# First block's modulation sums on TensorE, small vectors on the weights' queue, and w_in chunks issued a chunk ahead

## The chip, the cores and the metric

The kernel runs on one core of a Trainium2 chip. The metric is device time in microseconds. TensorE is called PE, VectorE DVE, ScalarE ACT, GpSimdE POOL, and SyncE, which issues most DMAs, SP.

## What is computed

One layer of a streaming encoder for 256 tokens of width 2048, in float32. Cut to what matters here:

```python
mod = silu(c) @ ada_w + ada_b                    # 2048 -> 6 x 2048
shift1, scale1, gate1, shift2, scale2, gate2 = split(mod)
h = rmsnorm(x, norm1_g) * (1 + scale1) + shift1
proj = h @ w_in                                  # 2048 -> 9216
u, v, q, k, v_b, gates = split(proj)
y_a = spatial_gating(gelu(u), gelu(v), gmlp_w_s, gmlp_b_s, ...) @ w_branch_a
y_b = band_attention(q, k, v_b, rel_bias) @ w_branch_b
x = x + gate1 * ((sigmoid(gates_a) * y_a + sigmoid(gates_b) * y_b) @ w_out)
h = rmsnorm(x, norm2_g) * (1 + scale2) + shift2
x = x + gate2 * moe(h)                           # 32 SwiGLU experts, two for each token
out = rmsnorm(x, final_g)
```

## The kernel before

The stages come in this order: a start (small vectors, x, its norm and transposes), the first part of the projection (five targets q, k, v_b, v, u of 1024 columns), the gates of the projection, the two branches, the output projection, the router, and the experts, whose weights (12.6 MB each) stream in one after the other.

The first part goes in four blocks (`BLOCKS = (4, 4, 4, 4)`). A block is four groups of 128 rows of w_in, because `h` can only be made for the columns whose shift and scale are known. In a block, `run_steps` is called for each of the five targets: it loads one chunk of w_in (128 x 4 x 1024, 2 MB, L111) and makes four steps. A step splits 128 x 1024 weights into a high part (ACT, L318) and a low part (DVE, L319), each in one of two buffers, and makes 12 products of 512 columns (L292 high x high, L293 low x high, L294 high x low). A block has 20 steps, 240 products. The partial results are copied (first block, ACT, L351) or added (DVE, L353).

While the products of one block run, the modulations of the next block are made by the generator `ada_block`, of which `run_steps` takes one step at each chunk and at each split (25 calls a block, 23 steps of the generator). It loads 2048 rows of ada_w, the shift and scale columns of the block, in four pieces of 2 MB (two DMAs each, L195), multiplies them with silu(c) and accumulates on DVE (L205 once, L207 15 times), sums over the partitions by transposes on PE and a reduce on DVE (L217, L220), adds the biases (L223 to L225), and makes `hx`, its high part `hh` and its low part `hl` (L230, L233 on ACT, L234 on DVE). The modulations of the first block are made by the same code ahead of the first chunk.

All these loads take the buffers r0 to r3 in turn (`raws`), and SP issues them one after the other; a load waits until the work on the load four before it is done. In the program a block's order is chunk, piece, chunk, piece, chunk, piece, chunk, piece, chunk. The order of instructions on an engine is set by a scheduler that goes by a model of when each is ready; it need not be the program's order, except where `issue_after` or `keep_in_program_order` says so.

In the last block the modulations of the rest (`ada_units`, L435) run in the place of `ada_block`. The router's stage holds a sum over one half of the last gate that is made by PE alone (`gate_steps`, L990): float32 matmuls with 64 equal columns of silu(c) as stationary operand and 512 columns of ada_w as moving one, two of them for two halves of the partitions of one bank. The experts' products are L1279, L1361 and L1393.

At the start c, norm1_g, two rows of ada_b and gmlp_b_s go by ACT's queue into one tile `rows` that PE turns (L169, L171), x goes by the same queue in two halves (L164), gmlp_w_s by POOL's (L167) and is turned ahead of the first block (L269, L270). ACT squares x (L251), scales it (L254) and copies the transposes of x (L259) to `hx` (L264).

Of the kernel before, what the change touches and what calls it, by code (L numbers as in the profile page):

```python
# [17 lines left out]
P = 128  # L18
S = 256
# [27 lines left out]
def hybrid_block(  # L47
# [69 lines left out]
    pending = []  # L117

# [22 lines left out]

    ident = T([P, P], "ident")
# [8 lines left out]
    rows = T([P, P], "a2")  # L151
    nc.vector.memset(rows, 0.0)
    r0 = 0
# [12 lines left out]
    for i in range(2):  # L166
        nc.gpsimd.dma_start(out=ws[i], in_=gmlp_w_s[0, 4 * i : 4 * i + 4].rearrange("g t s -> t g s"))  # L167
# [5 lines left out]
    nc.scalar.activation(sc, cols[:, 0:ND], AF.Silu)  # L173
# [13 lines left out]
    def ada_block(k0, n):  # L187

        w = n * P
        acc = accs.sb([P, 2, w])  # L190
        nj = 16 // n
        for j0 in range(0, ND, nj):
            rw = raws.sb([P, nj, 2, w])
            for m in range(2):
                nc.sync.dma_start(  # L195
                    out=rw[:, :, m, :],
                    in_=ada_w[
                        0, j0 * P : (j0 + nj) * P, m * D + k0 * P : m * D + k0 * P + w
                    ].rearrange("(j p) n -> p j n", p=P),
                )  # L200
            yield
# [12 lines left out]
        for m in range(2):  # L214
# [8 lines left out]
        nc.vector.tensor_add(sh1[:, ks], sums[:, 0, :], b_shift[:, ks])  # L223
        nc.vector.tensor_add(sg1[:, ks], sums[:, 1, :], b_scale[:, ks])
        nc.vector.scalar_tensor_tensor(  # L225
            out=sg1[:, ks], in0=sg1[:, ks], scalar=1.0, in1=g1c[:, ks], op0=ALU.add, op1=ALU.mult
        )
        yield
        for j in range(k0, k0 + n):
# [5 lines left out]
            if j % 2 == 1:  # L235
                yield

# [9 lines left out]
    first = ada_block(0, BLOCKS[0])  # L247
    ss1 = T([P, NT], "ss1")
    scr = T([P, D], "e2")
    for t in range(NT):  # L250
        nc.scalar.activation(scr, xt[t], AF.Square, accum_out=ss1[:, t : t + 1])  # L251
    rs1 = inv_rms(ss1, "n1")
    for t in range(NT):
        nc.scalar.activation(xt[t], xt[t], AF.Copy, scale=rs1[:, t : t + 1])  # L254
    for j in range(0, ND, 2):
        tp = bk.ps()
# [7 lines left out]
        nc.scalar.copy(hx[:, j : j + 2, :], tp.rearrange("p (a b) -> p a b", a=2))  # L264
    wsT = T([P, 8, P], "f3")
    for i in range(2):
        tp = bk.ps()
        for g in range(4):
            nc.tensor.transpose(tp[:, g * P : (g + 1) * P], ws[i][:, g, :], ident)  # L269
        nc.scalar.copy(wsT[:, 4 * i : 4 * i + 4, :], tp.rearrange("p (a b) -> p a b", a=4))  # L270
    nc.gpsimd.memset(wsT[CH:P, :, 0:CH], 0.0)
    for _ in first:
        pass


    def run_steps(lh, ll, w, k0, n, c0, evac, with_ada=None, cw=CW, after=None):

        nhf = cw // 512
        npc = 4096 // cw
        pt = []  # L280
# [24 lines left out]
        for q in range(k0, k0 + n, npc):  # L305
            m = min(npc, k0 + n - q)
            rw = load([P, m, cw], w[q * P : (q + m) * P, c0 : c0 + cw].rearrange("(j p) n -> p j n", p=P))
            if with_ada is not None:
                next(with_ada, None)
            for jj in range(m):  # L310
# [6 lines left out]
                def prepare(wh=wh, wl=wl, src=rw[:, jj, :]):  # L317
                    nc.scalar.copy(wh, src)  # L318
# [175 lines left out]
    for b, n in enumerate(BLOCKS):  # L494
        lastb = b == len(BLOCKS) - 1
        nxt = ada if lastb else ada_block(k0 + n, BLOCKS[b + 1])
# [7 lines left out]
        for c0, dst, func in homes:  # L504
            done = lastb and c0 == homes[-1][0]
            run_steps(
                lh_h, ll_h, win, k0, n, c0, home_evac(dst, func, b == 0, lastb), with_ada=nxt,
                after=(lambda: sides.append(both())) if done else None,
            )
        if not lastb:  # L510
            for _ in nxt:
                pass
        k0 += n
# [1091 lines left out]
```

## Time and profile before

| | us |
|---|---|
| median of 3 runs (1688.21 to 1690.66) | 1690.38 |
| the profiled execution's own time | 1689.86 |
| its span | 1688.1 |
| PE busy, share of the span | 1538.8, 91% |
| DVE busy | 942.5, 56% |
| ACT busy | 483.5, 29% |
| first product of the first block (L292) | 44.92 |

The span goes from the first to the last instruction of the profiled execution; its own time has 1.8 us around it. A busy share is an average over stages that have different limits.

### The profile page before, as it was taken

How to read it: one execution, taken by the hardware profiler on the slowest of the kernel's cores; microseconds unless marked ns; L12 is line 12 of the kernel's file. 1: busy time of each engine (PE TensorE's matmuls, PEld its weight loads, DVE VectorE, ACT ScalarE, POOL GpSimd, SP SyncE). 2: the span in 40 equal slices, each digit the busy share in tenths (PEclk: the TensorE clock that was granted, in tenths of full speed). 3: DMA queues.
4: the chain of work that ended last, by engine and by line, in shares of the span. 5: the costliest groups of instructions: out<-in, count | busy, mean ns of one | idle time of the engine just before them, and what ended most of it. 6: DMA issues, size and time to landing. Idle time of an engine off the chain costs nothing.

```text
span 1688.1 us, 18245 instructions
## 1 busy us (share of the span) xinstructions
PE 1538.8 (91%) x6725; PEld 856.1 (51%) x6725; DVE 942.5 (56%) x1313; ACT 483.5 (29%) x785; POOL 126.3 (7%) x377
## 2 busy tenths in 40 slices
PE   2999999999999999999998989989899898898996
PEld 1777778777887776643333323334233333332432
DVE  5789999998778888734332333323333233332334
ACT  4554345675444345341110111101111011110112
POOL 1000000000000000011100101001011010100101
PEclk8999999999999999999999999999999999999998
DMA  9989897797988786899999999999999999999996
GB/s 359 343 315 341 336 341 299 296 343 273 351 313 315 305 312 244 343 384 418 416 418 417 416 418 416 417 418 416 418 416 418 418 416 418 416 417 417 416 419 245
DMA packets 135358, 625.25 MB, mean 370 GB/s; under 512 B 5720, under 2 KB 5840, under 8 KB 101856
## 3 DMA queue, kind: packets, MB, share of 16 engines
q1 hardware_dynamic: 132832, 614.49, 91.5%
q10 hardware_dynamic: 992, 5.28, 0.8%
q0 software_dynamic: 1440, 4.27, 0.8%
q8 instruction: 55, 0.90, 0.2%
q14 instruction: 39, 0.32, 0.0%
HBM read 621.91 MB, written 2.10 MB: 370 GB/s over the span
## 4 chain that ended last, share of the span: by engine, by line
PE 51%; DMA 42%; DVE 4%; issue 2%; ACT 1%; SPq 0%; POOL 0%; POOLq 0%; DVEq 0%; ACTq 0%
DMA r<-in_w_dram 22%; PE b L1279 12%; PE b L294 11%; PE b L292 11%; PE b L293 10%; DMA dC<-in_w_dram 9%; DMA E<-in_w_dram 8%; PE b L1361 3%; DMA r<-in_ada_w_dram 2%; DVE W L319 1%; DVE f L435 1%; PE b L1393 1%; DVE f L207 0%; PE b L1183 0%; PE b L593 0%
## 5 line engine op out<-in xcount | busy, mean ns | idle before, releaser
L1279 PE MATMUL b<-r,e 128*64 128x512 f32 x1024 | 376.3, 626 | 44.2 <-DMA r<-in_w_dram 43.6
L1395 DVE TENSOR_TENSOR dB<-dB,b 128x512 f32<-128x512 f32 x248 | 153.6, 681 | 317.4 <-PE b L1393 317.4
L318 ACT CAST W<-r 128x1024 fp32r<-128x1024 f32 (+1 forms) x224 | 220.8, 987 | 328.6 <-PE b L293 294.0
L319 DVE TENSOR_TENSOR W<-r,W 128x1024 fp32r<-128x1024 f32 (+1 forms) x224 | 255.8, 1147 | 64.5 <-ACT W L318 63.2
L292 PE MATMUL b<-W,dC 128*128 128x512 f32 x704 | 284.9, 405 | 5.3 <-ACT dC L233 3.7
L293 PE MATMUL b<-W,dD 128*128 128x512 f32 x704 | 280.0, 398 | 0.0
L294 PE MATMUL b<-W,dC 128*128 128x512 f32 x704 | 267.1, 398 | 2.3 <-DVE W L319 2.1
L1385 ACT CAST f<-f 64x512 fp32r<-64x512 f32 x124 | 76.4, 616 | 576.2 <-DVE dB L1395 414.2
L1279 PEld LDWEIGHTS b<-r,e 128*64 128x64 f32 x1024 | 116.7, 144 | 215.9 <-issue 144.1
L292 PEld LDWEIGHTS b<-W,dC 128*128 128x128 f32 x704 | 132.9, 189 | 40.8 <-ACT dC L233 4.1
L294 PEld LDWEIGHTS b<-W,dC 128*128 128x128 f32 x704 | 131.5, 188 | 38.9 <-DVE W L319 8.0
L435 DVE SCALAR_TENSOR_TENSOR f<-r,sc,f 128x1024 f32<-128x1024 f32 x115 | 147.2, 1281 | 4.5 <-DMA r<-in_ada_w_dram 3.7
L293 PEld LDWEIGHTS b<-W,dD 128*128 128x128 f32 x704 | 132.7, 189 | 30.4 <-issue 0.5
L1279 PE MATMUL b<-dC,e 128*64 128x512 f32 x256 | 120.0, 624 | 19.6 <-DMA dC<-in_w_dram 19.6
L1279 PE MATMUL b<-E,e 128*64 128x512 f32 x256 | 118.2, 616 | 19.4 <-DMA E<-in_w_dram 19.4
L1279 PE MATMUL b<-dD,e 128*64 128x512 f32 x256 | 127.2, 648 | 0.0
L1352 DVE TENSOR_TENSOR f2y<-f2y,b 128x256 f32<-128x256 f32 x31 | 13.1, 421 | 198.6 <-ACT f2y L1351 198.6
L1279 PE MATMUL b<-W,e 128*64 128x512 f32 x256 | 121.8, 625 | 0.0
L1361 PE MATMUL b<-r,f2y 128*64 128x512 f32 x496 | 111.3, 595 | 0.0
L1386 DVE TENSOR_TENSOR f<-f,f 64x512 fp32r<-64x512 f32 x124 | 85.1, 686 | 26.4 <-ACT f L1385 23.5
L1294 POOL COPY e<-a 128x64 f32 x256 | 68.7, 271 | 205.0 <-PE b L1279 191.1
L207 DVE SCALAR_TENSOR_TENSOR f<-r,sc,f 128x1024 f32<-128x1024 f32 x60 | 77.0, 1283 | 1.6 <-DMA r<-in_ada_w_dram 1.0
(321 smaller groups left out, 1475.5 us busy)
## 6 DMA issues: line engine op xcount, KB each, us to landing
r<-in_w_dram SPq DMA_DIRECT2D x93, 2048.0 KB, 28.2
r<-in_w_in_dram SPq DMA_DIRECT2D x36, 2048.0 KB, 8.4
r<-in_ada_w_dram SPq DMA_DIRECT2D x32, 2048.0 KB, 8.6
W<-in_w_dram SPq DMA_DIRECT2D x23, 2048.0 KB, 28.5
dC<-in_w_dram SPq DMA_DIRECT2D x23, 2048.0 KB
dD<-in_w_dram SPq DMA_DIRECT2D x23, 2048.0 KB, 28.2
E<-in_w_dram SPq DMA_DIRECT2D x23, 2048.0 KB, 28.1
r<-in_ada_w_dram SPq DMA_DIRECT2D x32, 1024.0 KB, 10.1
```

Source lines behind the costliest of these rows:

```text
L207: nc.vector.scalar_tensor_tensor(out=acc, in0=rw[:, jj], scalar=sc[:, j : j + 1], in1=acc, op0=ALU.mult, op1=ALU.add,)
L292: nc.tensor.matmul(o, a, wh[:, cs], start=(k == k0), stop=False)
L293: nc.tensor.matmul(o, b, wh[:, cs], start=False, stop=False)
L294: closed[0] = nc.tensor.matmul(o, a, wl[:, cs], start=False, stop=close)
L318: nc.scalar.copy(wh, src)
L319: nc.vector.tensor_sub(wl, src, wh.bitcast(F32))
L435: nc.vector.scalar_tensor_tensor(out=acc, in0=rw[:, jj, :], scalar=sc[:, j : j + 1], in1=acc, op0=ALU.mult, op1=ALU.add,)
L1279: nc.tensor.matmul(pab[a * CH : (a + 1) * CH, :], xe[:, 8 * half + j, :], w[:, j // JQ, j % JQ, :], start=(half == 0 and j == 0), stop=(ha ...
L1361: nc.tensor.matmul(po[a * CH : (a + 1) * CH, :], act[:, j, :], w[:, j, a * 512 : (a + 1) * 512], start=(j == 0), stop=(j == 3),)
L1385: pin(nc.scalar.copy(oh[r, a, :], og[r, b, :]))
L1386: pin(nc.vector.tensor_sub(oh[o, a, :], og[r, b, :], oh[r, a, :].bitcast(F32)))
L1395: pin(nc.vector.tensor_add(xa[:, t, d0 : d0 + 512], xa[:, t, d0 : d0 + 512], pr))
```

## The change

The first block's sums are made by PE alone, in the manner of L990 (`ada_first`): silu(c), repeated in 64 columns, is the stationary operand, a piece of ada_w the moving one, and shift and scale land in two halves of one bank. The sums are then equal on 64 partitions; a matmul with a two-column `pick` turns them into columns. `hh` is made from `hx` directly by one ACT pass, `hl` by two DVE passes, the first group of 128 rows ahead of the other three.

c, norm1_g and ada_b (in one DMA) go first on SP's queue, gmlp_b_s on POOL's, x first on ACT's. x is scaled by DVE, the copies of its transposes alternate between ACT and DVE and use six banks. A Silu of two elements stands ahead of the real one.

The first quarter of the first w_in chunk is loaded ahead of the first block's last piece, the rest behind it. In the first part each chunk is issued one chunk earlier in the program, ahead of the piece of modulations beside it (`follow`, `fetched`). gmlp_w_s is loaded (by ACT's queue) and turned after the first block, beside the products of the second (`turn_ws`, one step at each step of products).

```diff
@@ start
+    casts = []
+    fetched = []
...
-    for src in (
-        c[0].rearrange("(j p) -> j p", p=P),
-        norm1_g[0].rearrange("(j p) -> j p", p=P),
-        ada_b[0, 0:D].rearrange("(j p) -> j p", p=P),
-        ada_b[0, D : 2 * D].rearrange("(j p) -> j p", p=P),
-        gmlp_b_s[0],
-    ):
-        nc.scalar.dma_start(out=rows[r0 : r0 + src.shape[0], :], in_=src)
-        r0 += src.shape[0]
     for t in range(NT):
         nc.scalar.dma_start(out=xt[t], in_=x[0, t * P : (t + 1) * P, :])
-    ws = [T([P, 4, P], "a0"), T([P, 4, P], "a1")]
-    for i in range(2):
-        nc.gpsimd.dma_start(out=ws[i], in_=gmlp_w_s[0, 4 * i : 4 * i + 4].rearrange("g t s -> t g s"))
+    r0 = 0
+    for src, queue in (
+        (c[0].rearrange("(j p) -> j p", p=P), nc.sync),
+        (norm1_g[0].rearrange("(j p) -> j p", p=P), nc.sync),
+        (ada_b[0, 0 : 2 * D].rearrange("(j p) -> j p", p=P), nc.sync),
+        (gmlp_b_s[0], nc.gpsimd),
+    ):
+        small = queue.dma_start(out=rows[r0 : r0 + src.shape[0], :], in_=src)
+        if queue is nc.sync:
+            small_last = small
...
+    nc.scalar.activation(mhalf[:, 1:2], mhalf[:, 0:1], AF.Silu)
+    nc.vector.memset(mhalf[:, 1:2], -0.5)
...
+    def ada_first(n):
+        w = n * P
+        scb = T([P, ND, CH], "f4")
+        nc.vector.tensor_copy(scb, sc.unsqueeze(2).to_broadcast([P, ND, CH]))
+        pick = T([P, 2], "pick")
+        nc.vector.tensor_copy(pick[:, 0:1], ident[:, 0:1])
+        nc.vector.tensor_copy(pick[:, 1:2], ident[:, CH : CH + 1])
+        pacc = bk.ps()
+        for j0, nj, rw in ada_pieces(0, n):
+            for jj in range(nj):
+                j = j0 + jj
+                for m in range(2):
+                    nc.tensor.matmul(
+                        pacc[m * CH : (m + 1) * CH, 0:w], scb[:, j, :], rw[:, jj, m, :],
+                        start=(j == 0), stop=(j == ND - 1),
+                    )
+            yield
+        part = T([P, w], "f0")
+        nc.scalar.copy(part[:, 0:P], pacc[:, 0:P])
+        nc.vector.tensor_copy(part[:, P:w], pacc[:, P:w])
+        for k0, k1 in ((0, 1), (1, n)):
+            tp = sk.ps()
+            for i in range(k0, k1):
+                nc.tensor.matmul(
+                    tp[:, 2 * (i - k0) : 2 * (i - k0) + 2], part[:, i * P : (i + 1) * P], pick,
+                    start=True, stop=True,
+                )
+            modulation(slice(k0, k1), tp[:, 0 : 2 * (k1 - k0)].rearrange("p (a b) -> p b a", b=2))
+            for j in range(k0, k1):
+                s, b = sg1[:, j : j + 1], sh1[:, j : j + 1]
+                nc.scalar.activation(hh[:, j, :], hx[:, j, :], AF.Identity, bias=b, scale=s)
+                full = scr[:, j * S : (j + 1) * S]
+                nc.vector.tensor_scalar(full, hx[:, j, :], s, b, op0=ALU.mult, op1=ALU.add)
+                nc.vector.tensor_sub(hl[:, j, :], full, hh[:, j, :].bitcast(F32))
+        yield
...
-    first = ada_block(0, BLOCKS[0])
+    first = ada_first(BLOCKS[0])
+    with tc.issue_after(small_last.ins):
+        next(first)
...
-        nc.scalar.activation(xt[t], xt[t], AF.Copy, scale=rs1[:, t : t + 1])
+        nc.vector.tensor_scalar(xt[t], xt[t], rs1[:, t : t + 1], None, op0=ALU.mult)
...
+    with tc.issue_after(small_last.ins):
+        next(first)
+        next(first)
+        early = [raws.sb([P, 4, CW])]
+        nc.sync.dma_start(out=early[0][:, 0, :], in_=w_in[0, 0:P, 2 * GW : 2 * GW + CW])
+        for _ in first:
+            pass
...
+    def turn_ws():
+        ws = [T([P, 4, P], "a0"), T([P, 4, P], "a1")]
+        with tc.issue_after(casts[-1].ins):
+            for i in range(2):
+                nc.scalar.dma_start(out=ws[i], in_=gmlp_w_s[0, 4 * i : 4 * i + 4].rearrange("g t s -> t g s"))
+        yield
+        for i in range(2):
+            tp = sk.ps()
+            for g in range(4):
+                nc.tensor.transpose(tp[:, g * P : (g + 1) * P], ws[i][:, g, :], ident)
+            nc.scalar.copy(wsT[:, 4 * i : 4 * i + 4, :], tp.rearrange("p (a b) -> p a b", a=4))
+            yield
...
@@ run_steps
-            rw = load([P, m, cw], src)
+            if early:
+                rw = early.pop()
+                tc.keep_in_program_order(nc.sync.dma_start(out=rw[:, 1:m, :], in_=src[:, 1:m, :]))
+            elif fetched:
+                rw = fetched.pop()
+            else:
+                rw = load([P, m, cw], src)
+            if follow is not None:
+                nk, nn, nc0 = follow
+                fetched.append(
+                    load([P, nn, cw], w[nk * P : (nk + nn) * P, nc0 : nc0 + cw].rearrange("(j p) n -> p j n", p=P))
+                )
             if with_ada is not None:
                 next(with_ada, None)
...
+            if h + 1 < len(homes):
+                follow = (k0, n, homes[h + 1][0])
+            elif not lastb:
+                follow = (k0 + n, BLOCKS[b + 1], homes[0][0])
...
+        if b == 0:
+            sides.append(turn_ws())
```

`ada_of` and `hurried`, which now hand out the steps of `ada_block`, and the new count of row groups in a load come to the same as before for blocks of four.

## Rows read from the trace of the kernel before

**Rows 1.** The page, part 4: shares of the chain that ended last.
```profile
PE 51%; DMA 42%; DVE 4%; issue 2%; ACT 1%; SPq 0%; POOL 0%; POOLq 0%; DVEq 0%; ACTq 0%
```

**Rows 2.** Windows: us, busy PE, PEld, DVE, ACT, POOL (instructions), clock, DMA, GB/s.
```profile
720.00:1616.00 896.00, 810.94 (x3454) 311.96 (x3452) 305.47 (x515) 128.77 (x256) 94.01 (x320) 0.97 1.01 416
```

**Rows 3.** The same columns: two windows of 11 us in the projection.
```profile
111.00:122.00 11.00, 11.00 (x49) 8.84 (x48) 9.20 (x11) 4.00 (x5) 0.00 (x0) 1.00 0.73 270
...
166.00:177.00 11.00, 11.00 (x49) 8.83 (x48) 11.00 (x12) 4.17 (x4) 0.00 (x0) 1.00 0.41 143
```

**Rows 4.** Waits of PE, 45 to 720 us, then 45 to 270: total, times, longest.
```profile
PE b L294 <- DVE W L319: 4.3, 6, 1.7
...
PE b L294 <- DVE W L319: 1.5, 2, 1.2
```

**Rows 5.** The chain that ended last, 0 to 60 us: start, us, what.
```profile
18.29 14.49 DMA r<-in_ada_w_dram
...
32.90 1.30 DVE f L207
...
40.16 1.23 DVE W L319
...
43.23 0.17 DVE sg L225
...
43.48 1.09 ACT dB L230 x2
...
44.92 0.80 PE b L292
...
50.28 0.24 PE b L292
```

**Rows 6.** Windows around the first product, columns as in rows 2.
```profile
29.20:32.00 2.80, 0.00 (x0) 0.00 (x0) 2.73 (x3) 1.51 (x4) 0.52 (x1) 1.00 1.06 391
...
33.00:38.00 5.00, 0.00 (x0) 0.00 (x0) 4.89 (x4) 0.07 (x1) 0.00 (x0) 0.50 1.02 403
...
44.90:49.90 5.00, 4.98 (x12) 3.85 (x13) 4.93 (x8) 1.87 (x5) 0.00 (x0) 0.50 1.03 398
50.00:56.00 6.00, 6.00 (x28) 4.81 (x27) 3.29 (x3) 2.41 (x3) 0.00 (x0) 1.00 0.55 199
```

**Rows 7.** DMA view, 0 to 60 us: GB/s in 1.5 us slots, and the software queue.
```profile
GB/s 0 164 396 369 380 314 226 373 411 376 386 386 386 386 388 386 386 388 386 386 386 412 407 410 396 388 386 388 408 407 412 393 390 388 385 142 11 79 333 423
...
q0 software_dynamic: 256, 0.55, 3.1%
```

**Rows 8.** Timeline: start, us, engine, line, operation, tiles, shapes, count [idle].
```profile
702.73 0.64 PE L1020 MATMUL b<-E 128*128 128x36 f32 x4 [0.53 <-DVE E L1016]
...
703.29 5.37 PE L990 MATMUL b<-r,E 128*64 128x512 f32 x24
...
9.84 0.29 DVE L171 COPY cols<-b 128x128 f32<-128x128 f32 x1 [8.66 <-PE b L169]
```

**Rows 9.** Timeline and DMA view: transposes and load of gmlp_w_s.
```profile
28.10 1.04 PE L269 MATMUL b<-ident,a 128*128 128x128 f32 x8
...
a<-in_gmlp_w_s_dram POOLq DMA_DIRECT2D x2, 256.0 KB, 7.5
```

**Rows 10.** SP's issues, then the DMA view, 45 to 230 us.
```profile
89.70 0.92 SPq L195 DMA_DIRECT2D r<-in_ada_w_dram  x2
...
159.20 0.92 SPq L195 DMA_DIRECT2D r<-in_ada_w_dram  x2
...
r<-in_w_in_dram SPq DMA_DIRECT2D x15, 2048.0 KB, 8.1
```

**Rows 11.** ACT's first issues; the group L207, 45 to 270 us (busy, mean | idle).
```profile
0.76 0.43 ACTq L164 DMA_DIRECT2D x<-in_x_dram  x1
1.24 0.43 ACTq L161 DMA_DIRECT2D a<-in_c_dram  x1
...
L207 DVE SCALAR_TENSOR_TENSOR f<-r,sc,f 128x1024 f32<-128x1024 f32 x45 | 57.7, 1283 | 0.2
```

More of the change, by code (lines that the diff above doesn't have):

```diff
@@ L139, in flush @@
             tick()
+    rows = T([P, P], "a2")
+    nc.vector.memset(rows, 0.0)
     ident = T([P, P], "ident")
@@ L200, in ada_block, with modulation @@
                 )
+            yield j0, nj, rw
+    def modulation(ks, sums):
+        nc.vector.tensor_add(sh1[:, ks], sums[:, 0, :], b_shift[:, ks])
+        nc.vector.tensor_add(sg1[:, ks], sums[:, 1, :], b_scale[:, ks])
+        nc.vector.scalar_tensor_tensor(
+            out=sg1[:, ks], in0=sg1[:, ks], scalar=1.0, in1=g1c[:, ks], op0=ALU.add, op1=ALU.mult
+        )
[34 more added lines that the diff above has]
+        yield
+    def ada_block(k0, n):
+        w = n * P
+        acc = accs.sb([P, 2, w])
+        for j0, nj, rw in ada_pieces(k0, n):
             yield
@@ L222, in ada_block @@
             )
[L223 to L227, printed above, removed]
+        modulation(ks, sums)
         yield
@@ L234, in ada_block, with ada_of, hurried @@
             nc.vector.tensor_sub(hl[:, j, :], hx[:, j, :], hh[:, j, :].bitcast(F32))
-            if j % 2 == 1:
+            if (j - k0) % 2 == 1 or j == k0 + n - 1:
                 yield
+    def ada_of(k0, n, calls):
+        parts = [n] if n <= 4 else [3, n - 3]
+        blocks, steps = [], 0
+        for m in parts:
+            blocks.append(ada_block(k0, m))
+            steps += (4 if m > 2 else 2) + ND + 1 + (m + 1) // 2
+            k0 += m
+        return hurried(itertools.chain(*blocks), max(1.0, steps / calls))
+    def hurried(g, rate):
+        due = 0.0
+        while True:
+            due += rate
+            while due >= 1.0:
+                due -= 1.0
+                if next(g, "end") == "end":
+                    return
+            yield
     def inv_rms(ss, name):
@@ L245, in inv_rms @@
         return rs
[L247 removed]
+    first = ada_first(BLOCKS[0])
+    with tc.issue_after(small_last.ins):
+        next(first)
     ss1 = T([P, NT], "ss1")
     scr = T([P, D], "e2")
[L250 to L251 removed]
+    with tc.issue_after(sc_made.ins):
+        for t in range(NT):
+            nc.scalar.activation(scr, xt[t], AF.Square, accum_out=ss1[:, t : t + 1])
     rs1 = inv_rms(ss1, "n1")
     for t in range(NT):
[L254 removed]
+        nc.vector.tensor_scalar(xt[t], xt[t], rs1[:, t : t + 1], None, op0=ALU.mult)
+    turned = Ring(["b2", "b3", "b4", "b5", "b6", "b0"])
     for j in range(0, ND, 2):
[L256 removed]
+        tp = turned.ps()
         for jj in range(2):
@@ L263, in hybrid_block, with run_steps @@
                 )
-        nc.scalar.copy(hx[:, j : j + 2, :], tp.rearrange("p (a b) -> p a b", a=2))
-    wsT = T([P, 8, P], "f3")
[L266 to L276, printed above, removed]
+        tv = tp.rearrange("p (a b) -> p a b", a=2)
+        if j % 4 == 0:
+            nc.scalar.copy(hx[:, j : j + 2, :], tv)
+        else:
+            nc.vector.tensor_copy(hx[:, j : j + 2, :], tv)
+    with tc.issue_after(small_last.ins):
[5 more added lines that the diff above has]
+            pass
+    wsT = T([P, 8, P], "f3")
+    def turn_ws():
[9 more added lines that the diff above has]
+            nc.scalar.copy(wsT[:, 4 * i : 4 * i + 4, :], tp.rearrange("p (a b) -> p a b", a=4))
+            yield
+        nc.gpsimd.memset(wsT[CH:P, :, 0:CH], 0.0)
+        yield
+    def run_steps(lh, ll, w, k0, n, c0, evac, with_ada=None, cw=CW, after=None, follow=None):
         nhf = cw // 512
         npc = 4096 // cw
+        npc = -(-n // -(-n // npc))
         pt = []
```

24 lines of the change are left out of this document (12 added, 12 removed).

## Prediction

> **What bounds the kernel now.** I read the page first: the chain that ended last is half TensorE (PE) and 42% DMA [rows 1]. The windows by stage say where each rules. From 720 to 1616 us the DMA engines are full, 416 GB/s for 896 us; this is the stream of expert weights [rows 2]. Before that PE rules: in each 11 us window of the projection it is busy for all 11 us [rows 3], and its waits between 45 and 720 us are few and short [rows 4]. The stream's first loads wait for buffers that the earlier stage gives back, so a microsecond saved at the start moves the stream, and the end, by about a microsecond. The change touches the first 215 us only: what it is worth is read at the first product (L292) and at the ends of the four blocks.
>
> The chain of the first 60 us [rows 5] shows what the first product waits for. The last piece of the first block's modulation weights lands at 32.8; four products on VectorE (DVE) follow, 1.30 each; then the transposes and sums (L217, L220), with a split of w_in (L319, 1.23) between them; then ScalarE (ACT); L292 starts at 44.92. From the landing to there it takes 12.1 us. Of the products after that, 12 take the 5.0 us to 49.9, 0.42 each [rows 6]; from 50.28 one takes 0.24 or 0.23, 0.233 on average. The windows give the reason: the granted clock fell to 0.50, the level of 1.2 GHz, at about 33, when PE had done nothing since 29.2, and came back to 1.00 (2.4 GHz) at about 50, when PE had worked from 44.9 on [rows 6].
>
> **The change, part by part.** The sum is made against the profiled execution's own 1689.86 us (span 1688.1 and 1.8 around it); the median shown is 0.5 above it.
>
> *The landing.* In front of the last piece the small-packet load of gmlp_w_s is taken away and 0.5 MB of w_in is put in. The software queue, nearly all of it gmlp_w_s, took 3.1% of 16 engines over 60 us, 1.9 us [rows 7]; 0.52 MB at the 0.386 MB/us of the same row of GB/s cost 1.35. So the landing comes 0.5 earlier, at 32.3, as the two shares give it. Bounds: 31.4, if the slots at 226 and 314 GB/s [rows 7] fill up too, and 34.1, if only the added bytes count. The x loads and the small vectors move between queues, but their bytes stay ahead of the last piece in either order: nothing. The last piece reuses the first one's buffer, whose matmuls end some 10 us before the queue could reach that piece: nothing.
>
> *The sums.* The last piece's four DVE products (5.25) go, and PE gets 8 float32 matmuls, 64 columns stationary, 512 moving, on two halves of the partitions. The kernel has this very form at L990: 12 matmuls, 24 records, 5.37 us [rows 8], so 0.45 each, and 8 take 3.6. At half clock it would be 7.2; these are the bounds. The matmuls of the three earlier pieces lie in the wait for the DMAs: nothing. They, and the transposes of x, keep PE at work from about 13 to 29 us.
> The Trainium skill (FP8 and Floating Point Precision, "TensorE Precision Notes") says that true FP32 takes four passes through the array. L990 shows two records for a matmul, so by the row it takes two. With four the last piece would cost 7.2 and the sum would be 3.6 later.
>
> *From the sums to L292.* Before: 38.2 to 44.92, 6.7. After: a copy of 128x128 out of PSUM (0.29 for the like, L171), a matmul that picks two columns (two matmuls with 36 columns took 0.64, so 0.32), three small vector operations (0.16 each), one ACT pass over 128x256 (1.09 for two, so 0.55) that writes the high part directly [rows 5, 8], and an estimated 0.1 at each of five handovers: 2.1. Splits of w_in become ready at the same time, and one stood in this stretch before; I add 0.5. With 2.6, L292 starts at 32.3 + 3.6 + 2.6 = 38.5, 6.4 earlier. Bounds 2.1 to 3.7 (a whole split in the way). The low part of the first column block and the other three blocks' modulations run under the first 12 matmuls (2.8 us) on DVE and ACT.
>
> *The clock.* Before, 12 records between 44.9 and 49.9 took 5.0 us, where 12 x 0.233 is 2.8 (a step of 12 takes 2.8, a chunk of four steps 11.2) [rows 3, 6]: some 2.2 lost, with the half products at the edges 2.3. After, the third piece lands at 25.5 (32.3 less 2.6 MB) and its matmuls end at 29.1; half of the last piece is there at 29.6, and its first matmul needs no more. PE's gaps are then under 3 us, shorter than the one in which the clock fell, so I expect full clock at the sums and at L292: 2.3 gained. Together 8.7.
>
> *The first weights.* L292 needs one quarter of the first chunk, which is ahead of the last piece; the rest lands 1.5 MB later, at 36.4, and the second chunk at 41.8, where PE wants it at 47. The third is wanted at 58.7 (two chunks of 11.2 us, less 2.2 for its cast and split); behind two pieces of modulations it lands at 58.1, behind one at 52.7. Hidden, if narrowly; with the landing at its bad bound, 34.1, it would be 1.2 us late.
>
> *The transposes of gmlp_w_s* move from an idle PE into the second block's stream: 8 took 1.04 [rows 9]. Their load took 7.5 us to land [rows 9] and is now issued at a cast on ACT; PE comes to the transposes one or two steps of 2.8 us later and, going in order, would stand there for the rest, 0 to 4 us. On ACT the issues and two copies cost nothing: it is busy 4.2 of 11 us there [rows 3]. I take 1.0 + 0.3: the cast runs a step ahead of PE, so that most of the landing is covered.
>
> *Chunks ahead of modulations.* From the third on, each w_in chunk waits for the last split of the chunk two before it, as it does already. What changes is the buffer, and so the wait, of the first two modulation pieces that the second and third blocks work off. Before, the first was issued 13 us ahead of its block (89.70 for the second block, which starts at 44.9 + 2.3 + 240 x 0.233 = 103.1), the second at its start (159.20 for the third) [rows 10]. After, the first waits for the last split of the fifth chunk (5.6 us ahead of the block), the second for that of the block's own first chunk (8 us into it); at 8.1 us from issue to landing [rows 10] it is there 16 us into the block, and DVE's products of it are due at 10 to 11. Until then DVE has splits and PSUM adds, some 4 us of work. It is busy 9.2 of 11 us early in the second block and 11.00 of 11 later [rows 3], so idle time there comes back as a wait of PE at the block's end. I take 0.5 for each of the two blocks, 1.0; bounds 0 and 5.6 (the second rival).
>
> The other moves (x scaled on DVE, half of the copies on DVE, one activation table early) lie in the wait for the weights: nothing, and if that cover went they would add up to the 2 to 4 us of such work that stands ahead of the last copy.
>
> Sum: -8.7 + 1.0 + 0.3 + 1.0 = -6.4; 1689.9 - 6.4 = 1683.5, or 1684.0 against the median. Its own range, with the bounds of the landing, the handovers and gmlp_w_s: 1680.5 to 1686.5.
>
> **The rivals.**
> *Half clock at the last sums.* PE idles between pieces, as between 29.2 and 33 before [rows 6]. Then 8 matmuls take 7.2, L292 starts at 42.1, at full clock since PE has worked for 7 us: the gain is 3.6 less, 1687.6. Against it: three pieces instead of none keep PE at work. The Trainium skill (TensorE: Matmul & The Clock Gate, "Part 1: The HAM clock gate") says that the throttled state is the default and activity lifts it; the trace agrees, 0.50 after the idle stretch and 1.00 after the busy one. By the four passes that the Trainium skill states (FP8 and Floating Point Precision, "TensorE Precision Notes") the time would be the same, 1687.6, without the clock; L990 speaks against it.
>
> *The gain is taken back at the ends of the second and third blocks.* If DVE idles 3 to 4 us in a block because a piece is late, the sums for the next block end as much later, and PE waits at the boundary. One wait of 1.2 us for L319 is there already [rows 4]. Price 3 to 4 less 1.2, for two blocks 3.6 to 5.6 where I took 1.0: 1687.6 on average.
>
> *Slower.* SP issues in order. If the issue order is that of the program, a piece stands behind a chunk that waits for its buffer: the chunk lands 8.1 us after that split [rows 10] and the piece 5.4 later, while DVE has the piece's products between two splits and comes to them after some 4. It stands there for 9.5, the second split buffer covers 2.8, PE waits 6.7. From two such waits on (13.4 against the 6.4) the change is slower; two in each of the second and third blocks give 1684 + 27 = 1711. Against it: instructions don't run in the program's order here. On ACT the load of x was issued ahead of that of c, which the program has first [rows 11], and in the chain a split of the later code, L319 at 40.16, stands ahead of the last sums [rows 5]; and DVE's products of the pieces (L207) stood idle 0.2 us in all in the blocks [rows 11].
>
> *It does not do what it says:* the weights' order saves nothing, because each chunk from the third on waits for the same split as before. That is so in my sum, where all of the gain is at the start: 1684.0, with the first case.
>
> **How the numbers follow.** 0.2% is 3.4 us, about what a measurement of this kernel can tell from none: faster is below 1687.0, slower above 1693.8. As forecast 0.58; half clock 0.15 (the four passes 0.02 of it); taken back 0.17; slower 0.10. The predicted time is that of the first. Faster: the first but for 0.02, and a third of the second and third: 0.56 + 0.05 + 0.06 = 0.67. Slower 0.10. The same is the rest, 0.23. The range reaches from the first case's good end to the third's bad one, 1680.5 to 1689.5, and leaves out the slower case and tails of the others.
>
> **What would show it.** L292 first at 38 to 39 with starts 0.23 apart at once; the last piece's 16 records on PE in 3.6 us; the granted clock 1.00 from 30 to 50; 8 transposes of gmlp_w_s after the first block, with a wait under 1 us ahead of them; the ends of the second and third blocks some 7 us earlier than before, and the full DMA windows too. A first product after 41, a granted clock of 0.50 at 33, a wait of PE for L319 or L234 of over 2 us at a block's end, or of DVE for a piece of modulation weights, would prove a step wrong.

## Result, and the profile after

The changed kernel takes 1707.14 us (median of 4, 1706.01 to 1707.41), the kernel before 1690.25 beside it: ratio 1.0102, 95% interval 1.0089 to 1.0115. It is 17 us slower; 1684.0 was forecast. One of the ten executions of f2 (below) took 5631 us and is left out of its ratio.

The start came out as forecast. The chain that ended last, 18 to 45 us, has the last piece landed at 32.37, its sums done 3.7 us later, the first product (now L387; L388 and L389 are the other two) at 38.03:

```profile
20.63 11.74 DMA r<-in_ada_w_dram
...
32.41 3.66 PE b L226 x14
...
37.23 0.81 PE b L237 x6
...
40.36 0.43 PE b L388
...
44.26 0.23 PE b L389
```

That is 6.9 us earlier than [rows 5] has it. But the products begin at half clock, 0.43 each until 42 us. The windows (columns as in [rows 2]) put it beside the granted clock, which is 1.00 through the sums and falls behind them:

```profile
34.00:36.00 2.00, 2.00 (x8) 0.42 (x4) 0.00 (x0) 0.00 (x0) 0.00 (x0) 1.00 1.00 397
36.00:38.00 2.00, 1.21 (x9) 1.04 (x8) 0.85 (x4) 0.89 (x3) 0.00 (x0) 1.00 1.06 422
38.00:40.00 2.00, 1.62 (x5) 1.06 (x5) 1.86 (x8) 1.72 (x3) 0.00 (x0) 0.68 1.00 399
40.00:42.00 2.00, 2.00 (x6) 1.52 (x6) 2.00 (x5) 0.77 (x2) 0.00 (x0) 0.50 1.03 387
42.00:44.00 2.00, 2.00 (x10) 1.64 (x9) 0.39 (x2) 1.05 (x1) 0.00 (x0) 0.96 1.05 387
```

The loss is further on. This table, worked out from the traces, has the starts of some products: 0, 240, 480 and 720 open the four blocks, 960 follows the fourth, 1200 and 2064 lie in the stages up to the experts. The last column is the span.

```
product       0    240    480    720    960   1200   2064     span
before      44.9  105.0  163.2  221.8  281.1  358.5  580.3   1688.1
after       38.0  107.7  172.2  232.6  295.0  375.3  595.8   1704.2
```

The first block takes 69.6 us where it took 60.1, the second 64.6 (58.2), the third 60.4 (58.5), the fourth 62.4 (59.4). The expert stream is the same, later by what came before it (window as in [rows 2]):

```profile
720.00:1616.00 896.00, 812.03 (x3459) 322.12 (x3457) 311.49 (x558) 127.73 (x253) 93.29 (x316) 0.96 1.01 415
```

PE's waits from 45 to 720 us (in all, times, longest), against those of [rows 4]: L427 is the split, L362 the transposes of gmlp_w_s, L426 the cast on ACT.

```profile
PE b L389 <- DVE W L427: 14.8, 13, 2.6
PE b L362 <- DMA a<-in_gmlp_w_s_dram: 5.7, 1, 5.7
PE b L387 <- ACT W L426: 3.2, 4, 1.6
```

The wait at the end of the first block is put down to gmlp_w_s. PE's timeline there (products left out) shows more: the transposes of the sums (L271) also come late, at 99.17. DVE's last step of the modulations (L284, `hl`) follows from 104.1 to 106.4; gmlp_w_s landed at 106.8.

```profile
99.17 0.63 PE L271 MATMUL b<-ident,f 128*128 128x128 f32 x4 [0.51 <-DVE f L261]
100.58 0.66 PE L271 MATMUL b<-ident,f 128*128 128x128 f32 x4 [0.79 <-DVE sums L274]
106.93 1.09 PE L362 MATMUL b<-ident,a 128*128 128x128 f32 x4 [5.69 <-DMA a<-in_gmlp_w_s_dram]
```

```profile
104.10 0.76 DVE L284 TENSOR_TENSOR dD<-dB,dC 128x256 fp32r<-128x256 f32 x2 [0.32 <-ACT dC L283]
105.69 0.76 DVE L284 TENSOR_TENSOR dD<-dB,dC 128x256 fp32r<-128x256 f32 x2 [0.83 <-ACT dC L283]
```

The second block's first products need only the first of these, so gmlp_w_s holds PE for the last 2 to 3 us of the 5.7, the modulations for what is ahead of that. After the wait PE also runs slower: 0.66 of the clock is granted over the next 5 us, by which about 1.7 us are lost (0.34 of 5.0, an estimate).

```profile
107.00:112.00 5.00, 5.00 (x17) 4.13 (x18) 0.00 (x0) 0.82 (x2) 0.00 (x0) 0.66 0.45 163
```

The transposes of the sums wait for DVE's products of the pieces (L259 once, L261). DVE's timeline: it stands idle between the splits early in the block and works off the last piece just ahead of the end.

```profile
49.58 1.23 DVE L427 TENSOR_TENSOR W<-r,W 128x1024 fp32r<-128x1024 f32 x1 [1.57 <-ACT W L426]
52.39 1.23 DVE L427 TENSOR_TENSOR W<-r,W 128x1024 fp32r<-128x1024 f32 x1 [1.59 <-ACT W L426]
53.54 0.75 DVE L259 TENSOR_SCALAR f<-r,sc 128x1024 f32<-128x1024 f32 x1
...
91.15 1.23 DVE L427 TENSOR_TENSOR W<-r,W 128x1024 fp32r<-128x1024 f32 x1 [1.61 <-ACT W L426]
92.29 1.28 DVE L261 SCALAR_TENSOR_TENSOR f<-r,sc,f 128x1024 f32<-128x1024 f32 x1
93.95 1.23 DVE L427 TENSOR_TENSOR W<-r,W 128x1024 fp32r<-128x1024 f32 x1 [0.38 <-ACT W L426]
95.10 3.92 DVE L261 SCALAR_TENSOR_TENSOR f<-r,sc,f 128x1024 f32<-128x1024 f32 x3
```

SP's issues show where the pieces (L197) went: each leaves just behind a chunk (L111) that waited for its buffer.

```profile
48.03 0.37 SPq L111 DMA_DIRECT2D r<-in_w_in_dram  x1
48.50 1.00 SPq L197 DMA_DIRECT2D r<-in_ada_w_dram  x2
59.23 0.37 SPq L111 DMA_DIRECT2D r<-in_w_in_dram  x1
60.43 1.27 SPq L197 DMA_DIRECT2D r<-in_ada_w_dram  x2
```

In the trace of after the four pieces of this block are landed at 47.9, 61.0, 73.5 and 84.3, and DVE's first products of them start at 53.5, 67.5, 79.2 and 92.3, 6 to 8 us behind the landing, while DVE stands idle between splits. Before, the last piece is landed at 79.9, and its products start 6.0 behind that:

```profile
85.94 2.60 DVE L207 SCALAR_TENSOR_TENSOR f<-r,sc,f 128x1024 f32<-128x1024 f32 x2
```

So they are late twice. Counted from the first product of the block, the last piece is landed 46.3 us into it (35.0 before), and its own first product starts 54.3 us into it (41.0 before).

### The profile page after: what moved, and what is told of

Read it like the earlier page. It is cut to its first block, busy times and chain, and to the rows that moved or that the text cites. A ratio compares the mean times of both kernels' runs of the same rounds, so it can differ in the third digit from the quotient of the medians.

```text
span 1704.2 us, 18356 instructions
## 1 busy us (share of the span) xinstructions
PE 1557.7 (91%) x6789; PEld 867.7 (51%) x6789; DVE 929.4 (55%) x1313; ACT 476.9 (28%) x776; POOL 125.4 (7%) x376
## 4 chain that ended last, share of the span: by engine, by line
PE 48%; DMA 43%; DVE 5%; issue 2%; ACT 1%; SPq 0%; POOLq 0%; POOL 0%; DVEq 0%; ACTq 0%
DMA r<-in_w_dram 22%; PE b L1394 12%; PE b L389 10%; PE b L387 9%; PE b L388 9%; DMA dC<-in_w_dram 9%; DMA E<-in_w_dram 8%; DMA r<-in_ada_w_dram 3%; PE b L1476 3%; DVE W L427 1%; DVE f L261 1%; PE b L1508 1%; DVE E L461 1%; PE b L226 1%; DMA a<-in_gmlp_w_s_dram 0%
## 5 line engine op out<-in xcount | busy, mean ns | idle before, releaser
L1394 PE MATMUL b<-r,e 128*64 128x512 f32 x1024 | 372.7, 622 | 39.3 <-DMA r<-in_w_dram 38.7
L426 ACT CAST W<-r 128x1024 fp32r<-128x1024 f32 (+1 forms) x224 | 220.9, 988 | 332.9 <-PE b L388 295.2
L427 DVE TENSOR_TENSOR W<-r,W 128x1024 fp32r<-128x1024 f32 (+1 forms) x224 | 255.2, 1145 | 81.5 <-ACT W L426 80.3
L387 PE MATMUL b<-W,dC 128*128 128x512 f32 x704 | 283.2, 404 | 3.2 <-ACT W L426 3.2
L388 PE MATMUL b<-W,dD 128*128 128x512 f32 x704 | 280.4, 398 | 0.4 <-DVE dD L247 0.4
L389 PE MATMUL b<-W,dC 128*128 128x512 f32 x704 | 267.7, 400 | 12.4 <-DVE W L427 12.3
L389 PEld LDWEIGHTS b<-W,dC 128*128 128x128 f32 x704 | 131.2, 189 | 51.1 <-DVE W L427 20.4
L387 PEld LDWEIGHTS b<-W,dC 128*128 128x128 f32 x704 | 132.6, 189 | 38.9 <-ACT W L426 5.5
L543 DVE SCALAR_TENSOR_TENSOR f<-r,sc,f 128x1024 f32<-128x1024 f32 x115 | 147.2, 1280 | 4.1 <-DMA r<-in_ada_w_dram 3.4
L388 PEld LDWEIGHTS b<-W,dD 128*128 128x128 f32 x704 | 132.9, 189 | 31.6 <-DVE dD L247 0.8
L1394 PE MATMUL b<-E,e 128*64 128x512 f32 x256 | 122.9, 636 | 22.6 <-DMA E<-in_w_dram 22.6
L1394 PEld LDWEIGHTS b<-dC,e 128*64 128x64 f32 x256 | 36.0, 145 | 91.6 <-issue 59.8
```

Source lines behind the costliest of these rows:

```text
L387: nc.tensor.matmul(o, a, wh[:, cs], start=(k == k0), stop=False)
L388: nc.tensor.matmul(o, b, wh[:, cs], start=False, stop=False)
L389: closed[0] = nc.tensor.matmul(o, a, wl[:, cs], start=False, stop=close)
L426: casts.append(nc.scalar.copy(wh, src))
L427: nc.vector.tensor_sub(wl, src, wh.bitcast(F32))
L543: nc.vector.scalar_tensor_tensor(out=acc, in0=rw[:, jj, :], scalar=sc[:, j : j + 1], in1=acc, op0=ALU.mult, op1=ALU.add,)
```

## Experiments

The first theory, A: the pieces come a chunk late because SP issues them behind the chunks, in the program's order; so the sums are late at each block's end. Its rival, W: the wait for gmlp_w_s is the main loss. The first four kernels are the 2 x 2 of the two parts (the whole change is one of its four cells), and gmlp_w_s turned later. The kernel before, measured again beside each group of runs, had medians of 1688.8 to 1690.3, so one microsecond between kernels of different groups says little.

**e1, gmlp_w_s at the start.** Load and transposes stand ahead of the first block as before.

```diff
+    for i in range(2):
+        nc.gpsimd.dma_start(out=ws[i], in_=gmlp_w_s[0, 4 * i : 4 * i + 4].rearrange("g t s -> t g s"))
...
-        if b == 0:
-            sides.append(turn_ws())
```

> Undone: gmlp_w_s is loaded by POOL's queue and turned ahead of the first block, as before the change; the rest of the change stays. Theory A (the pieces of modulations come a chunk late, because SP issues them behind the chunks in the program's order): only the wait of PE for gmlp_w_s (5.7 us), its eight transposes (1.0) and the half clock after it come back, less 1.3 for 0.5 MB back ahead of the last piece: 1700 to 1703, and the second block still ends with a wait for its sums. Theory W (the wait for gmlp_w_s is the main loss, and the lateness of the blocks after it follows from it): 1688 to 1695.

Measured: 1707.45 us, ratio 1.0102 (1.0086 to 1.0119), as with the whole change. PE still waits at the end of the first block, now with the right name; its waits from 80 to 125 us begin:

```profile
PE b L378 <- ACT dC L286: 4.0, 1, 4.0
PE b L378 <- ACT W L417: 1.6, 1, 1.6
```

(L286 makes `hh`.) W falls. A's number was missed too. The first block is 2.4 us shorter and the second 1.1, but the start lost 4.7 (first product at 42.8), where A reckoned with 1.3: the load is ahead of the last piece again, and the sums ran partly at half clock. So nothing came back in all.

**e2, pieces in their old order.** gmlp_w_s stays in the second block.

```diff
-            follow = None
-            if h + 1 < len(homes):
-                follow = (k0, n, homes[h + 1][0])
-            elif not lastb:
-                follow = (k0 + n, BLOCKS[b + 1], homes[0][0])
+            follow = None
```

> Undone: each chunk of the first part is issued in its own place again, ahead of its block's piece but behind the piece before it; gmlp_w_s stays in the second block. Theory A: the blocks' ends get their sums in time again, and what stays of the loss is the wait for gmlp_w_s, 1690 less 7 for the start, plus 1 to 6: 1685 to 1690. Theory W: the wait for gmlp_w_s stays with all that it draws behind it, 1698 to 1703.

Measured: 1693.78, ratio 1.0027 (1.0017 to 1.0036). 13 us come back, but 4 to 9 less than A wanted. PE's wait for gmlp_w_s is 1.7 here.

**e3, the new start only**: both edits together.

> Both undone: gmlp_w_s at the start and the chunks in their old order; the new sums on PE and the small vectors first on SP's queue stay. Both theories: the gain at the start is kept, first product at 39 to 40, 1683 to 1686. If it is not below 1687, the start itself gives its gain back later and neither theory holds.

Measured: 1692.76, ratio 1.0021 (1.0011 to 1.0031). By the last sentence of the expectation the start gives its gain back, and neither theory holds as it was put. First product 41.3 (3.6 earlier than before), second block 107.3 (2.3 later). The chunks' new place costs 14.7 us (e1 against e3) or 13.4 (the whole change against e2); where gmlp_w_s stands makes 0.3 to 1.0. e2 and e3 lose at another place: PE stands 1.8 us at each of four chunk boundaries of the first block. On ACT the four copies out of PSUM (L459) stand ahead of the next chunk's casts (e2, ACT's timeline):

```profile
49.61 2.68 ACT L459 COPY E<-b 128x512 f32<-128x512 f32 x4 [2.69 <-PE b L389]
52.19 2.00 ACT L426 CAST W<-r 128x1024 fp32r<-128x1024 f32 x2
```

The chunk had landed at 47.9. With the chunks' new place the first two of these four waits are not there, and the third is 0.4 us. That the copies cause them is theory C.

**e4, gmlp_w_s turned later.**

```diff
-        yield
+        for _ in range(5):
+            yield
         for i in range(2):
             tp = sk.ps()
```

> The transposes of gmlp_w_s come five steps of products after its load instead of one; its load stays where it is and the chunks stay ahead of the pieces. Theory A: PE no longer stands for gmlp_w_s, but the sums at the end of the first block are late as before, 1700 to 1704. Theory W: 1688 to 1695.

Measured: 1709.14, ratio 1.0115 (1.0098 to 1.0131). Four of the eight transposes stood in the same gap, with a wait of 7.0, so this edit did not do what it says, and tells little.

**f1, the new start and the casts first**: e3, and in the first block the copies are queued behind the newest cast.

```diff
             if begin:
-                nc.scalar.copy(o, p)
+                with tc.issue_after(casts[-1].ins):
+                    nc.scalar.copy(o, p)
```

> The new start alone (gmlp_w_s at the start, chunks in their old order), with one edit more: the first block's copies out of PSUM on ACT are queued behind the first cast of the next chunk, where the new start alone had them ahead of it. Theory C (the start gains 3.6 us up to the first product, and PE then stands 1.8 us at each of four chunk boundaries because four copies stand ahead of the cast on ACT): these waits go, the second block begins 6 to 8 us earlier than with the new start alone, 1684.5 to 1687. Rival (the chunk itself is late by its DMA): the waits stay, now for the DMA, 1691 to 1694.

Measured: 1689.40, ratio 1.0002 (0.9992 to 1.0012), 3.4 less than e3. The waits at the boundaries went from 1.8 to 1.1 or less and the second block begins at 104.6, 2.7 earlier; C has the right cause, but the median lies above its range: the price was under half of what I put (6 to 8).

**f2, no new place for the chunks, casts first**: e2 and e4's edit, and that of f1.

> All of the change but the chunks' new place; the same edit of ACT's queue; the transposes of gmlp_w_s five steps after its load. Theories A and C: the first product stays at 38.0, the blocks keep their 58 to 59 us, the wait for gmlp_w_s is gone, and the gain at the start is kept: 1681 to 1685, faster than before. Rival (the later stages take back whatever the start gives): 1687 or more.

Measured: 1686.65, ratio 0.9989 (0.9979 to 0.9999). The second block begins at 99.8, 5.2 earlier than before, and there is no wait for gmlp_w_s. The median lies between the theories' range and the rival's.

**f3, pieces on POOL's queue.**

```diff
-                nc.sync.dma_start(
+                (nc.gpsimd if k0 else nc.sync).dma_start(
                     out=rw[:, :, m, :],
```

> The whole change, but the pieces of modulations of the second to fourth blocks are issued by POOL's queue instead of SP's, so that none stands behind a chunk that waits for its buffer. Theory A (SP's order makes the pieces late): they land some 10 us earlier in the first block, PE's wait at its end goes, and of the 13 to 15 us that the chunks' new place costs most comes back: 1690 to 1697. Rival (the pieces are late for their buffers, or DVE has too much to do): 1703 to 1709. If POOL's issuing is slow, between.

Measured: 1707.37, ratio 1.0114 (1.0097 to 1.0131). The pieces are landed at 47.8, 53.4, 68.3 and 79.0, from the second on as early as before the change (the first was there at 43.3 then), and the wait for the sums at the end of the first block is gone. Yet nothing was won: A's range is missed, and the time lies in the rival's. PE's waits, 0 to 740 us, show a new one:

```profile
PE b L389 <- DVE W L427: 12.0, 12, 3.1
...
PE b L388 <- DVE dD L247: 6.2, 2, 5.9
```

DVE's queue has a product of the first piece ahead of the `hl` (L247) of the first block, and stands for the landing at 47.8. A alone cannot say why DVE's queue is now too early, and was too late in the changed kernel.

**f4, before and the chunks' new place**: `follow` and `fetched` as in the change, nothing else of it.

> The kernel before with one part of the change alone: each chunk of the first part issued one chunk earlier, ahead of the piece beside it. Theory A: the loss does not need the new start or the moved gmlp_w_s; 1700 to 1705. Rival (it needs the earlier first product, which gives DVE less time ahead): 1690 to 1695.

Measured: 1702.24, ratio 1.0083 (1.0066 to 1.0100), in A's range. The loss needs no new start. The first block keeps its 60.1 us here, though its last piece is landed only at 88.7; the second takes 63.2, the third 62.5.

I then read the order of DVE's queue in each trace: S is a split, p a product of the second block's pieces, counted from the first block's first split; four p are a piece, four S a chunk.

```
before S1 S2.p1.p2.p3.p4 S3 S4 S5.p5 S6.p6 S7.p7 S8.p8 S9 S10.p9 S11.p10.p11 S12.p12 S13 S14 S15.p13.p14 S16.p15.p16 S17
f2     S1 S2 S3 S4.p1.p2.p3.p4 S5 S6 S7.p5 S8.p6.p7.p8 S9 S10 S11.p9 S12.p10.p11.p12 S13 S14 S15.p13 S16.p14.p15.p16 S17
after  S1 S2 S3 S4 S5 S6.p1.p2 S7.p3 S8.p4 S9 S10 S11.p5.p6 S12.p7.p8 S13 S14 S15.p9 S16.p10.p11.p12 S17 S18 S19.p13 S20.p14.p15.p16 S21
f3     S1.p1 S2.p2 S3.p3 S4.p4 S5.p5 S6.p6 S7.p7.p8 S8.p9 S9.p10 S10.p11 S11.p12.p13 S12.p14 S13.p15 S14.p16 S15
```

Splits ahead of the last product: 16 before and in e2, e3, f1, f2; 20 in the changed kernel, e1 and e4; 19 in f4; 14 in f3. The queue was laid out a chunk later where the pieces stand behind the chunks. That is theory D: what DVE waits for is not the landing but the product's place in its own queue.

**g1, products earlier on DVE**: e4, and splits of the first block queued behind products.

```diff
+    early_by = {11: 6, 12: 8, 14: 9, 15: 11, 16: 12, 18: 14, 19: 15, 20: 16}
...
+                    first = early_by.get(len(casts))
...
+                        with tc.issue_after(prods_dve[first - 1].ins):
+                            nc.vector.tensor_sub(wl, src, wh.bitcast(F32))
```

> The whole change with gmlp_w_s turned later; the loads and their order stay. In the first block some splits on DVE are queued behind products of the pieces that stood behind them, so that the last piece's four products come one to two splits earlier, at once when it lands. Theory D (what is late is not the landing but the place that the products got in DVE's queue: the last of the 16 stands behind 20 splits, behind 16 in the kernel before, though its piece landed 8 us ahead of its first product): the second block begins at 101 to 104 instead of 109, 1701 to 1705. Theory A as it stood (DVE waits for landings): products queued earlier only wait, the second block begins at 107 or later, 1706 to 1710.

Measured: 1696.53, ratio 1.0041 (1.0027 to 1.0055): 12.6 less than e4, by an edit that changes the place of no load in the program. The last piece is landed at 85.0, no earlier than in after; its products (L263 here) start at once, with the splits (L433, L436) among them:

```profile
85.08 2.60 DVE L263 SCALAR_TENSOR_TENSOR f<-r,sc,f 128x1024 f32<-128x1024 f32 x2 [1.55 <-DMA r<-in_ada_w_dram]
87.60 1.22 DVE L436 TENSOR_TENSOR W<-r,W 128x1024 fp32r<-128x1024 f32 x1
88.74 1.28 DVE L263 SCALAR_TENSOR_TENSOR f<-r,sc,f 128x1024 f32<-128x1024 f32 x1
89.94 1.22 DVE L436 TENSOR_TENSOR W<-r,W 128x1024 fp32r<-128x1024 f32 x1
91.07 1.28 DVE L263 SCALAR_TENSOR_TENSOR f<-r,sc,f 128x1024 f32<-128x1024 f32 x1
```

The second block begins at 98.2 (109.3 in e4), and the first takes 60.2 us, as before (60.1). Better than D's own range. Part of it goes by gmlp_w_s: its load stands behind a cast on ACT, left 5.9 us earlier here (93.1 against 99.0), and e4's wait of 7.0 for it is gone. The modulations alone (the first `hh`) are ready 6.2 us earlier than in e4.

**g2, before with the products late on DVE**: each product queued behind the split four later.

```diff
+                    todo.append(product)
+                    if len(todo) > 4:
+                        with tc.issue_after(splits[-1].ins):
+                            todo.pop(0)()
```

> The kernel before with nothing changed but DVE's queue: every product of a piece of modulations is queued behind the split four splits later, so that the last of a block stands behind its 20th split, as in the changed kernel; loads and chunks as before. Theory D: the sums come 11 us later, 3.7 of which the first block has to spare; PE waits some 7 us at the end of each of the first three blocks, 1703 to 1712. Rival (the order on DVE matters little; what costs is the transfers' order): under 1694.

Measured: 1708.66, ratio 1.0112 (1.0095 to 1.0129). The chunks are where they were in the program, and still the loss is as large as that of the whole change. Each of the first three blocks ends with a wait of 3.5 to 3.6 for `hh` (L251 here), half of what I put; after the first of these waits the granted clock is 0.50 from 111 to 113 us. PE's waits, 45 to 270 us (the fourth is that ahead of the first product, as in the kernel before):

```profile
PE b L310 <- ACT dC L251: 14.4, 4, 3.7
```

Pieces leave later too, as their buffers come free later; but none of DVE's waits in these blocks is for one.

**g3, products spread**: f2, and g1's edit with other pairs.

```diff
+    early_by = {4: 2, 8: 6, 12: 10, 16: 14}
```

> The version without the chunks' new place and with the first casts first; in the first block a split in each chunk is queued behind two products of the piece, so that two stand ahead of it and two behind, where one and three stood. By theory D's reading of DVE's queue, three products in a row (3.9 us) make the next split late by some 0.4 to 1 us a chunk: second block 1 to 3 us earlier, 1683 to 1686. If the splits are not what PE waits for there, as without it, 1686 to 1687.

Measured: 1684.76, ratio 0.9970 (0.9958 to 0.9981), faster than both kernels. In DVE's timelines f2 has three products ahead of two splits, g3 two and two:

```profile
59.05 3.92 DVE L261 SCALAR_TENSOR_TENSOR f<-r,sc,f 128x1024 f32<-128x1024 f32 x3
62.89 2.56 DVE L428 TENSOR_TENSOR W<-r,W 128x1024 fp32r<-128x1024 f32 x2
```

```profile
58.91 1.22 DVE L436 TENSOR_TENSOR W<-r,W 128x1024 fp32r<-128x1024 f32 x1
60.04 2.60 DVE L263 SCALAR_TENSOR_TENSOR f<-r,sc,f 128x1024 f32<-128x1024 f32 x2
62.62 1.23 DVE L433 TENSOR_TENSOR W<-r,W 128x1024 fp32r<-128x1024 f32 x1
```

The second block begins 0.6 earlier than in f2, less than the 1 to 3 expected, though the first product ran at half clock here and not there.

**h1, chunks ahead in the first block only**: g1, and

```diff
-            if h + 1 < len(homes):
+            if b == 0 and h + 1 < len(homes):
                 follow = (k0, n, homes[h + 1][0])
-            elif not lastb:
-                follow = (k0 + n, BLOCKS[b + 1], homes[0][0])
```

> The version with products earlier on DVE, and the chunks one place ahead in the first block only; from the second block's first chunk on they are issued in their old places. Theory D with A for the later blocks (there the second to fourth pieces are landed only shortly before their products, because their buffers come free a chunk later): the second block begins at 98 to 100 as with products earlier on DVE, the blocks after it take the 58 to 59 us of before, 1683 to 1687. Rival (what is left of the loss comes from the first block or the start): 1693 to 1697.

Measured: 1686.65, ratio 0.9981 (0.9972 to 0.9990). So of the 11.8 us between g1 and g3, 9.9 came from the new place in the later blocks. There the landings are close to the products: in g1's second block the last three pieces are landed at 114.7, 128.4 and 140.4, the first products start at 118.1, 130.2 and 142.4. But DVE has no wait for a piece there either (98 to 225 us). So whether the landing binds in these blocks or the order of DVE's queue is not shown; no run moved one of them alone. By the landings the products could have come 1.8 to 3.4 us earlier.

The starts of products, as above:

```
product       0    240    480    720    960   1200   2064     span
e1          42.8  110.0  173.5  234.1  296.4  376.7  597.0   1705.9
e2          38.0  104.4  165.4  223.0  288.1  362.4  583.8   1691.9
e3          41.3  107.3  165.7  223.5  286.5  362.3  582.7   1691.8
f4          45.0  105.0  168.3  230.7  291.0  372.4  592.8   1701.0
g1          38.0   98.2  162.4  223.4  285.6  365.9  586.0   1693.8
g3          38.0   99.2  157.5  215.1  280.5  354.9  575.0   1683.1
h1          38.4   98.9  159.3  216.9  282.3  356.4  576.6   1684.7
```

## Why the prediction was wrong

**Landing, sums, handovers: right.** 32.4, 3.7 and 2.0 against 32.3, 3.6 and 2.6; first product 38.03 against 38.5. Inside the landing two errors cancel: with gmlp_w_s back at the start (e3) the last piece lands at 35.63 (22.94 and 12.69 in the row below), 3.3 later, where I had given 1.9; and w_in's 0.5 MB with the new order of the small loads costs 2.8 (32.8 to 35.63), where I had given 1.35.

```profile
22.94 12.69 DMA r<-in_ada_w_dram
```

The last piece's 16 records took 3.66 (14 are recorded), so a float32 matmul leaves two records here, 0.23 each: two passes, by the rows. The four passes that the Trainium skill states (FP8 and Floating Point Precision, "TensorE Precision Notes") are not seen in this trace.

**Clock: the direction was wrong for the first products.** Full clock at the sums, as forecast, but half at L387: the first 48 products take 13.3 us, 12.0 in f2, which keeps full clock: 1.3 of the 2.3 us are gone.

**gmlp_w_s: too small, but not by what its wait shows.** I put 1.0 for the transposes and 0.3 of waiting; the trace shows a wait of 5.7. Half of that stands beside the late modulations: in e1, which takes load and transposes away, the first two blocks are 3.5 us shorter together. At the start the load costs more than that, 4.7 at the first product. In e2, where the modulations are in time, a wait of 1.7 is left; in f2, with the transposes five steps later as well, there is none.

**Chunks ahead of modulations: the step that failed.** It went: what changes is the wait of the first two pieces of the second and third blocks, 0.5 each. Three things were wrong in it.

First, the first block, of which it says nothing, lost most: 69.6 us where g1, with the loads in the same places and another order on DVE, takes 60.2. That counts what gmlp_w_s costs there (2.4 by e1).

Second, I looked for lateness at a landing. In the changed kernel DVE has no wait for a piece from 45 to 240 us. DVE goes through its queue in the order in which it was laid out ahead of the run: with the first piece landed at 47.9 it stands idle twice for 1.6 us ahead of splits, and makes the first product at 53.5. That order has the products a chunk later as soon as the pieces are a chunk later on SP. With the loads left in their places in the program, another order on DVE gave back 12.6 us (g1) and took 18.7 (g2, from the median beside it). The evidence that I used against a delay, L207's idle time of 0.2 us [rows 11], cannot show one: such a queue seldom waits for a piece, it has the product later.

Third, in the second and third blocks the landings are late, as I said (in g1 the second piece is there 16.4 us into the second block, where I had reckoned 16; 5.7 before), but the price was 9.9 (h1 against g1) and not 1.0; whether the landings make it or DVE's order is open. The starts of the two blocks that I reckoned with, 103.1 and about 159, are 105.0 and 163.2 in the trace of before. I had seen that the second piece's buffer comes free 8 us into the block, and then took a value near the low end of 0 to 5.6.

**The slower rival was nearer than its chance of 0.10.** I argued that instructions don't run in the program's order. For SP's loads in the first block they did: each piece left right behind its chunk. Its price, 1711, was near; its mechanism, DVE standing for the landing with splits behind it, is what f3 shows in one place and not what the changed kernel does.

**A step that I had not taken: the copies on ACT.** "On ACT the issues and two copies cost nothing" looked at busy time. In e2 and e3 four copies ahead of a cast cost PE 1.8 us at each chunk, 7 in all; f1's edit brings 3.4 of it. So the new start alone is no gain, although its first product is 3.6 (e3) or 6.9 (e2) earlier.

**How much of a gain at the start arrives?** In g3 6.9 us at the first product are 5.8 at the second block, 6.7 at the fourth, 0.6 at product 960, 3.6 at 1200 and 5.0 in the span; by the medians 5.2. The forecast's -6.4 would have been about right with the queues in order, though the way to it differs. The fourth block takes 63 to 65 us in the versions with the new start and the old place of the chunks (59.4 before). In g3 all 32 transposes of q and k stand in it, where before has 12 in it and 20 behind product 960: work of PE other than products takes 5.7 us there (2.4 before) and waits 3.5 (0.8). From 960 to 1200 that work is 19.2 (23.4 before), and this is the half that comes back. Why PE's order is another there stays open.

## What to carry to other kernels

An edit to the order of transfers also moves the order in which each engine's queue is laid out: count, in the trace before and after, how many other instructions stand ahead of the last one that matters (16 against 20 here), not only what each waits for. The count is a hint and not the price: with 19 the first block lost nothing in f4 and g1, and with 14 it lost as much in f3. Where an engine keeps to a planned order, a delay can show as idle time ahead of something else (splits here) and as a wait at the next stage boundary, and not at its cause. A wait's name is that of the latest of several: before mending it, look for the second latest, which was 2 to 3 us ahead of it here, in a wait of 5.7.

## What the hardware showed

The clock fell to its lower level though PE never stood still for long. In the changed kernel PE's longest idle stretch from 15 us to the first products is the 1.56 us ahead of the last sums; 0.50 was granted from 38.7 to 42.2, in the first products. In e2, e3, e4, f3, g1, g3 and h1, with 1.04 to 1.64 us ahead of the last sums, it was the same; in f1, with 0.73, 0.50 came from 43.2 to 46.6; in f2, with 0.63, it stayed at 1.00. In e1, with 2.09, the sums already ran partly at half clock (14 records in 5.34 us).

```profile
35.47 5.34 PE L229 MATMUL b<-r,f 128*64 128x512 f32 x14 [2.09 <-DMA r<-in_ada_w_dram]
```

```profile
32.52 3.65 PE L226 MATMUL b<-r,f 128*64 128x512 f32 x14 [0.63 <-DMA r<-in_ada_w_dram]
```

Whether these stretches made the clock fall, or the thin one between the sums and the first products (PE busy 1.21 of 2.00 us from 36 to 38), no run shows. Either way, gaps "under 3 us" as in the forecast were not safe. The other surprise is gmlp_w_s: its queue took 3.1% of 16 engines over 60 us, 1.9 us, in e3 as in [rows 7], but the transfers behind it land 3.3 us later.
